# A transformer block with expert routing on one core: pool waits tile by tile, a rearranged start of the gate loop, and a third buffer for stored gates

## The chip, the cores and the metric

The kernel runs on one core of a Trainium2 chip. The metric is the device time of one execution in microseconds (us); lower is better. The engines are TensorE (PE, with its weight loads shown as PEld), VectorE (DVE), ScalarE (ACT), GpSimd (POOL) and SyncE (SP, which only issues transfers). SP, ACT and POOL each issue transfers from their own queue.

## The reference

`x` is 512 tokens of 1024 values. A first half mixes tokens, a second sends each token to experts:

```python
xn = rms_norm(x, ln_mix_g); proj = xn @ w_in
a_out = gmlp_spatial_gating(...)          # 8 groups, blocks of 128 tokens
b_out = banded_chunk_attention(...)       # 8 heads, relative bias
x = x + concat([a_out, b_out]) @ w_out
# PEER, per token, 8 heads: two 128-wide score rows, top 16 of each, best 16 of the sums
s_top, i_top = top_k(sc, 16); best, pos = top_k(pairwise sums, 16)
g = softmax(best); eidx = i0 * 128 + i1   # 16 of 16384 experts for each head
h = gelu(einsum(expert_u[eidx], xb))
out = x + einsum(g * h, expert_v[eidx])
```

## The kernel before

All arithmetic is float32; a product of float32 matrices is made as three fp32r products of a high and a low part (`mm3`, L190). The high part comes from an ACT copy (L154), the low part from a subtraction on DVE or POOL (L155), both in `load_split` (L146). It has three raw, five high and five low buffers.

The four token tiles of 128 are not treated alike. Tile 0 fetches its experts' rows by index ("gathers", L1105 to L1120). The other three tiles multiply with **all** 16384 experts: 128 blocks of 128 experts, two blocks to a chunk, 64 chunks. Of these three tiles, the last 64 tokens get their `expert_u` products by gathers too ("early" gathers, L649 to L669, 64 of them with the row product at L662), so the dense product over `expert_u` has only 320 columns (`multiply_some`, L690; one block is 24 matmuls). Its results wait in `act` tiles, 23 chunks ahead (`AHEAD`).

The order of the work is:

1. Mixing (to about 240 us), in pools `prea`, `preb`, `prec`, opened one after the other in the same memory.
2. Routing (240 to 427 us, loop at L882): for each head the query product, the score product, top 16, candidate sums, choice. Beside it the early gathers and some dense blocks run. `indices_early(h)` (L665) writes eight columns of one index tile `eui`, by a POOL transfer (L668) and a POOL cast (L669); six gathers follow each head's. At the end stand softmax (L796), `indices_of` (L862), two held splits, the last `indices_early`, and `dots_early(0)`, which orders all remaining row products.
3. The gate loop (L1017, 48 steps and 2 of lead, each for 8 tokens), in an order written out by hand for PE, DVE, ACT and POOL. A step makes a one-hot product `bm` on POOL (L963), a one-hot `am` on DVE (L971), 8 matmuls of `bm` and `am` (L979), two ACT copies into `gst` (L982), and after every two steps a 1 MB store to DRAM from the ACT queue (L986). `gst` has two buffers. Dense blocks, one early gather in two of three steps, and the row products stand between. A gate group is read back by `load_gates` (L991). The first two loads of it are POOL transfers.
4. The output (from about 592 us, L1182): for each chunk 36 matmuls of 512 columns into six PSUM banks (`second_product`, L1137), the dense blocks of the chunk 23 further on, and between them tile 0's routing (`route_gathered`, L1087, at every third chunk, eight times; its scores come by a transfer into `sc0`, one buffer) and tile 0's 256 gathers. DVE and ACT instructions are ordered by a planner with priorities, PE by hand.

Memory that a closed pool leaves is given to later pools. As written, the first use of it waits for the whole earlier pool's work. DMA issues of POOL use a descriptor scratch of 16 KB in each partition.

Of the kernel before, what the change touches and what calls it, by code (L numbers as in the profile page):

```python
# [80 lines left out]
GB = 8  # L81
TC = 8
# [10 lines left out]
def hybrid_block(tc, x, ln1, w_in, gng, wsT, bsb, qkg, bias, w_out, ln2, wq, skT, uT, ud, vd, out):  # L93
    nc = tc.nc
    ctx = ExitStack()
    with ctx:
# [26 lines left out]
        roots, behind_scale, behind_norm = [], [], []  # L123
# [22 lines left out]
        def load_split(src, eng=nc.vector, **dims):  # L146
# [125 lines left out]
        with tc.tile_pool(name="prea", bufs=1) as prea:  # L272
# [144 lines left out]
        with tc.tile_pool(name="preb", bufs=1) as preb:  # L417
# [163 lines left out]
        xbp = ctx.enter_context(tc.tile_pool(name="xbp", bufs=1, side="right"))  # L581
# [8 lines left out]
        with tc.tile_pool(name="prec", bufs=1) as preb:  # L590
# [27 lines left out]
        ps_x = ctx.enter_context(tc.tile_pool(name="ps_x", bufs=1, space=PSUM))  # L618
        ps_a = ctx.enter_context(tc.tile_pool(name="ps_b", bufs=4, space=PSUM))
# [5 lines left out]
        rt = ctx.enter_context(tc.tile_pool(name="rt", bufs=1, side="right"))  # L625
# [4 lines left out]
        actp = ctx.enter_context(tc.tile_pool(name="actp", bufs=1, side="right"))  # L630
# [4 lines left out]
        gat = gat_ctx.enter_context(tc.tile_pool(name="gat", bufs=1, side="right"))  # L635
        xbu = px()
        routing = ExitStack()
        rq = routing.enter_context(tc.tile_pool(name="rq", bufs=1))
# [5 lines left out]
        eui = gat.tile([P, HS], I32, name="eui")  # L644
# [4 lines left out]
        def gather_early(n, rows_of, n_rows):  # L649

            for j in early[:n]:
                row = rows_of.tile([P, D], F32, name="rowe", tag="rowe", bufs=n_rows)
                nc.gpsimd.indirect_dma_start(out=row, out_offset=None, in_=ud,  # L653
                                             in_offset=bass.IndirectOffsetOnAxis(ap=eui[:, j:j + 1], axis=0))
# [10 lines left out]
        def indices_early(h):  # L665

            js = slice(h * HK, (h + 1) * HK)
            nc.gpsimd.dma_start(eui[0:P - UX, js], eidx[P - UX:P, TT - 1, h * TOPK + HK:(h + 1) * TOPK])  # L668
            nc.gpsimd.tensor_copy(eui[P - UX:P, js], eidx[P - UX:P, TT - 1, h * TOPK:h * TOPK + HK])  # L669
# [212 lines left out]
        for h in range(NH + 1):  # L882
# [7 lines left out]
            if h > 1:  # L890
# [34 lines left out]
        indices_early(NH - 1)  # L925
        ready_early(NH - 1)
        dots_early(0)
# [5 lines left out]
        more.append(ctx.enter_context(tc.tile_pool(name="more", bufs=1)))  # L933
        gp_ctx = ExitStack()
        gp = gp_ctx.enter_context(tc.tile_pool(name="gp", bufs=1))
# [74 lines left out]
        with tc.manual_schedule(engines=engines):  # L1010
            gather_early(1, gat, ROWA)
# [5 lines left out]
            for n in range(steps + LEAD):  # L1017
# [31 lines left out]
                if n == own - 1:  # L1049
# [3 lines left out]
                    gcp = [ctx.enter_context(tc.tile_pool(name="gcp", bufs=1, side="right"))]  # L1053
# [24 lines left out]
        ep = ctx.enter_context(tc.tile_pool(name="ep", bufs=1))  # L1078
# [58 lines left out]
        def second_product(c):  # L1137
# [5 lines left out]
            for b in range(BC):  # L1143
                bb = (c * BC + b) % GB
                av = act[:, b, :].rearrange("p (n t) -> p n t", t=TG)
                nc.vector.tensor_tensor(av, av, gc[:, 0:NDU // TG, bb, :], op=ALU.mult)
            nc.scalar.activation(wh[:, :, 0:NDU], act, AF.Copy)
            mark = nc.vector.tensor_tensor(wl[:, :, 0:NDU], act, wh[:, :, 0:NDU].bitcast(F32), op=ALU.subtract)
            if c == 1:
# [98 lines left out]
```

## Time and profile before

| | |
|---|---|
| three runs | 1442.33 us median (1438.95 to 1442.57) |
| the profiled execution | 1436.48 us, of which the span from the first to the last instruction is 1434.4 us |
| granted TensorE clock over the span | 0.993 |
| busy share of the span | PE 97%, PEld 86%, DVE 80%, POOL 49%, ACT 43% |

All rows further down are of this one profiled execution. "Idle before" is time in which the engine did nothing ahead of an instruction, with what ended it; a wait is given as total, times, longest.

### The profile page before, as it was taken

To read this page: it belongs to the slowest core of one execution; us is meant where nothing else is said; L and a number is where in the kernel's file an instruction comes from. 1 tells how busy PE (TensorE), PEld (TensorE's weight loads), DVE (VectorE), ACT (ScalarE), POOL (GpSimd) and SP (SyncE) were. 2 spreads that over 40 slices of the span, in tenths; PEclk is the share of its full clock that TensorE was granted. 3 is DMA by queue.
4 is the path that set the end of the run, shared out by engine and by line. 5 is a ranking of instruction groups with operands and counts; after the bars stand their busy time and mean duration, and the time that the engine had idled before them with its cause. 6 is when DMAs were issued, how large, how long until landed. Compare 5 with 4: busy or idle time off the path is not lost.

```text
span 1434.4 us, 21711 instructions
## 1 busy us (share of the span) xinstructions
PE 1391.9 (97%) x7838; PEld 1229.5 (86%) x7838; DVE 1150.5 (80%) x2502; ACT 611.4 (43%) x957; POOL 700.6 (49%) x487
## 2 busy tenths in 40 slices
PE   9999999999987978999999999999999999999998
PEld 7887788898986978898988898998998998888887
DVE  5537755998996888599999999889879888688883
ACT  5447635434442434554543444343333333333331
POOL 0002104678769988424554646545546455254520
PEclk9999999999998999999999999999999999999999
DMA  4352225667667998988998999999999989689981
GB/s 168 126 191 74 89 104 191 206 229 276 216 225 248 300 313 251 294 296 310 332 351 312 339 349 368 347 389 356 376 339 359 361 326 378 243 326 353 340 332 70
DMA packets 164330, 396.24 MB, mean 276 GB/s; under 512 B 12880, under 2 KB 75232, under 8 KB 162176
## 3 DMA queue, kind: packets, MB, share of 16 engines
q1 hardware_dynamic: 64640, 194.14, 37.6%
q0 software_dynamic: 48176, 173.46, 32.9%
q10 hardware_dynamic: 51408, 27.27, 6.6%
q8 instruction: 61, 1.00, 0.3%
q14 instruction: 45, 0.37, 0.1%
HBM read 363.34 MB, written 31.46 MB: 275 GB/s over the span
## 4 chain that ended last, share of the span: by engine, by line
PE 76%; DVE 9%; POOL 5%; DMA 4%; issue 3%; ACT 2%; another core or an unknown queue 0%; ACTq 0%; POOLq 0%; DVEq 0%; SPq 0%
PE pa L1168 22%; PE px L1168 11%; PE pu L194 9%; PE pu L192 9%; PE pu L193 9%; PE pa L192 4%; PE pa L979 3%; PE pa L193 3%; PE pa L194 3%; POOL bm L963 2%; POOL rowe L653 1%; DMA gd<-gst 1%; DVE lo L155 1%; POOL lo L155 1%; DVE row L1109 1%
## 5 line engine op out<-in xcount | busy, mean ns | idle before, releaser
L154 ACT ACTIVATE hi<-raw 128x1024 fp32r<-128x1024 f32 x296 | 312.8, 1058 | 468.5 <-DMA raw<-in_vd 124.0
L155 DVE TENSOR_TENSOR lo<-raw,hi 128x1024 fp32r<-128x1024 f32 x241 | 295.8, 1229 | 78.3 <-ACT hi L154 76.0
L1107 POOL DMA_INDIRECT row<-in_ud,eint x128 | 199.0, 1555 | 193.6 <-DVE acc L1120 129.8
L1118 POOL DMA_INDIRECT row<-in_vd,eint x128 | 180.6, 1411 | 165.3 <-DVE row L1109 110.9
L194 PE MATMUL pu<-xch,lo 128*128 128x320 f32 x784 | 244.7, 312 | 8.1 <-POOL lo L155 4.9
L192 PE MATMUL pu<-xch,hi 128*128 128x320 f32 x784 | 248.9, 317 | 2.0 <-ACT act L716 2.0
L193 PE MATMUL pu<-xcl,hi 128*128 128x320 f32 x784 | 244.2, 311 | 0.0
L1168 PE MATMUL pa<-lo,wh 128*128 128x512 f32 x512 | 199.7, 390 | 0.0
L1168 PE MATMUL pa<-hi,wh 128*128 128x512 f32 x512 | 199.3, 389 | 0.0
L155 POOL TENSOR_TENSOR lo<-raw,hi 128x1024 fp32r<-128x1024 f32 x55 | 131.4, 2403 | 98.3 <-ACT hi L154 95.7
L1120 DVE SCALAR_TENSOR_TENSOR acc<-row,hw,acc 128x1024 f32<-128x1024 f32 x128 | 164.9, 1288 | 2.0 <-DMA row<-in_vd,eint 1.9
L1109 DVE SCALAR_TENSOR_TENSOR row<-row,xb 128x1024 f32<-128x1024 f32 x128 | 157.8, 1235 | 1.7 <-DMA row<-in_ud,eint 1.7
L1168 PE MATMUL pa<-hi,wl 128*128 128x512 f32 x512 | 158.4, 389 | 0.0
L194 PEld LDWEIGHTS pu<-xch,lo 128*128 128x128 f32 x784 | 149.2, 190 | 8.9 <-POOL lo L155 5.4
L192 PEld LDWEIGHTS pu<-xch,hi 128*128 128x128 f32 x784 | 149.5, 191 | 4.1 <-ACT act L716 2.5
L193 PEld LDWEIGHTS pu<-xcl,hi 128*128 128x128 f32 x784 | 149.5, 191 | 1.7
L979 PE MATMUL pa<-bm,am 128*128 128x128 f32 x768 | 97.3, 280 | 19.0 <-POOL bm L963 12.9
L1168 PEld LDWEIGHTS pa<-hi,wh 128*128 128x128 f32 x512 | 96.1, 188 | 20.6
L1168 PEld LDWEIGHTS pa<-lo,wh 128*128 128x128 f32 x512 | 96.1, 188 | 20.3
L1168 PEld LDWEIGHTS pa<-hi,wl 128*128 128x128 f32 x512 | 96.1, 188 | 20.2
L979 PEld LDWEIGHTS pa<-bm,am 128*128 128x128 f32 x768 | 92.2, 194 | 23.7 <-POOL bm L963 17.2
L1168 PE MATMUL px<-hi,wh 128*128 128x512 f32 x256 | 100.5, 393 | 3.3 <-ACT hi L154 3.3
(236 smaller groups left out, 2629.4 us busy)
## 6 DMA issues: line engine op xcount, KB each, us to landing
raw<-in_uT SPq DMA_DIRECT2D x128, 512.0 KB
raw<-in_vd SPq DMA_DIRECT2D x128, 512.0 KB
gd<-gst ACTq DMA_DIRECT2D x24, 1024.0 KB
gc<-gd SPq DMA_DIRECT2D x15, 1280.0 KB
raw<-in_w_in SPq DMA_DIRECT2D x19, 512.0 KB
raw<-in_wq SPq DMA_DIRECT2D x16, 512.0 KB
raw<-in_w_out SPq DMA_DIRECT2D x8, 512.0 KB
gc<-gd SPq DMA_DIRECT2D x15, 256.0 KB
```

Source lines behind the costliest of these rows:

```text
L154: nc.scalar.activation(hi, raw, AF.Copy)
L155: ins = eng.tensor_tensor(lo, raw, hi.bitcast(F32), op=ALU.subtract)
L192: nc.tensor.matmul(ps, lh[0], rh[0], start=first, stop=False)
L193: nc.tensor.matmul(ps, lh[0], rh[1], start=False, stop=False)
L194: nc.tensor.matmul(ps, lh[1], rh[0], start=False, stop=last)
L963: nc.gpsimd.tensor_tensor(bm.rearrange("p t (h l) -> p t h l", l=BL), d[0][:, ts_, :, None].to_broadcast(full), d[1][:, ts_, None, :].to_b ...
L979: nc.tensor.matmul(ps[:, i * P:(i + 1) * P], am[:, 4 * q + i, :], bm[:, 4 * q + i, :], start=True, stop=True)
L1107: nc.gpsimd.indirect_dma_start(out=row, out_offset=None, in_=ud, in_offset=bass.IndirectOffsetOnAxis(ap=eint[:, j:j + 1], axis=0))
L1109: nc.vector.scalar_tensor_tensor(row, row, 1.0, xb0, op0=ALU.mult, op1=ALU.mult, accum_out=hw[:, j:j + 1])
L1118: nc.gpsimd.indirect_dma_start(out=row, out_offset=None, in_=vd, in_offset=bass.IndirectOffsetOnAxis(ap=eint[:, j:j + 1], axis=0))
L1120: nc.vector.scalar_tensor_tensor(acc0, row, hw[:, j:j + 1], acc0, op0=ALU.mult, op1=ALU.add)
L1168: nc.tensor.matmul(accs[t][half], (wh, wh, wl)[k][:, b, tok], w[b][k % 2][:, ds_], start=first and k == 0, stop=last and k == 2)
```

## The change

Fourteen pools get `reuse_waits="tile"`: a tile in memory that an earlier pool left waits for the tiles whose bytes it takes, and no longer for the whole pool. `eui` becomes eight tiles, one for each head. The last pass of the routing loop no longer makes head 6's indices and issues no gathers, and behind it neither head 7's indices nor the remaining row products stand: the indices of both heads are made in steps 1 and 2 of the gate loop, six gathers are issued behind the last held split, the loop's gathers start at step 2 in three of four steps, and a step does at most one row product, from step 1 on. `gst` gets a third buffer, `sc0` a second, and the descriptor scratch shrinks to 4 KB. In chunk 0 of the output the products go by token tile, the dense blocks of chunk 23 are put ahead of the last token tile's, and the gates of the last tokens are split only there; the scaling products of chunks 1 to 3 are queued behind the chunk before.

```diff
+SCRATCH = 4096
@@ load_split
-            nc.scalar.activation(hi, raw, AF.Copy)
+            top = nc.scalar.activation(hi, raw, AF.Copy)
             ins = eng.tensor_tensor(lo, raw, hi.bitcast(F32), op=ALU.subtract)
+            halved[:] = [getattr(i, "ins", i) for i in (top, ins)]
@@ prea, preb, xbp, prec, ps_x, ps_b, rt, actp, gat, rq, more, gp, gcp, ep alike
-        with tc.tile_pool(name="prea", bufs=1) as prea:
+        with tc.tile_pool(name="prea", bufs=1, reuse_waits="tile") as prea:
@@ early gathers
-        eui = gat.tile([P, HS], I32, name="eui")
+        eui = [gat.tile([P, HK], I32, name=f"eui{h}") for h in range(NH)]
-        def dots_early(lag):
-            while len(issued) > lag:
+        def dots_early(lag, most=NH * HK):
+            while len(issued) > lag and most > 0:
+                most -= 1
@@ routing loop and its end
-            if h > 1:
+            if 1 < h < NH:
                 with tc.issue_after(splits[0]):
                     indices_early(h - 2)
                     ready_early(h - 2)
                     gather_early(EARLY, gat, ROWA)
@@
         for _ in range(HELD):
             split_next()
-        indices_early(NH - 1)
-        ready_early(NH - 1)
-        dots_early(0)
+        with tc.issue_after(splits[0]):
+            gather_early(EARLY, gat, ROWA)
@@ gate loop
-            gather_early(1, gat, ROWA)
             multiply_tile()
@@
-                        st = gp.tile([P, NB, TG], F32, name="gst", tag="gst", bufs=2)
+                        st = gp.tile([P, NB, TG], F32, name="gst", tag="gst", bufs=3)
@@
-                if n < own - 7 and n % 3 < 2:
+                if n in (1, 2):
+                    indices_early(NH - 3 + n)
+                    ready_early(NH - 3 + n)
+                if n:
+                    dots_early(LAGE, 1)
+                if 1 < n < own - 7 and n % 4 != 1:
                     gather_early(1, gat, ROWA)
-                dots_early(LAGE)
@@ route_gathered
-            sc = ep.tile([P, n, 2, NK], F32, name="sc0", tag="sc0", bufs=1)
+            sc = ep.tile([P, n, 2, NK], F32, name="sc0", tag="sc0", bufs=2)
@@ second_product(c, between)
+            with queued_behind(marked if c < GB // BC else []):
+                for b in range(BC):
+                    ...
+                    nc.vector.tensor_tensor(av, av, gc[:, 0:NDU // TG, bb, :], op=ALU.mult)
+            if c:
+                with queued_behind(own_last if c < GB // BC else []):
+                    last_tokens()
-            if c == NCHK - 1:
+            if c in (0, NCHK - 1):
                 order.sort(key=lambda bt: bt[1])
-            for b, t in order:
+            for i, (b, t) in enumerate(order):
+                if c == 0 and i == BC * (ND - 1):
+                    between()
+                    with queued_behind(halved):
+                        last_tokens()
@@ kernel
-    nc = bacc.Bacc("TRN2", target_bir_lowering=False, num_devices=1)
+    nc = bacc.Bacc("TRN2", target_bir_lowering=False, num_devices=1, dynamic_dma_scratch_size=SCRATCH)
```

`last_tokens()` holds the two instructions that split the gates of the last 64 tokens (L1157, L1158 before), and `between()` the dense blocks of the chunk 23 further on; for the other chunks both stand where they stood.

## Rows read from the trace of the kernel before

**Rows 1.** The head of the page: busy time and share of the span; and PE in 40 equal slices of 35.9 us, in tenths.

```profile
PE 1391.9 (97%) x7838; PEld 1229.5 (86%) x7838; DVE 1150.5 (80%) x2502; ACT 611.4 (43%) x957; POOL 700.6 (49%) x487
PE   9999999999987978999999999999999999999998
```

**Rows 2.** All waits of PE over the span that are 2.5 us or more in total: engine, tile and line, what it waited for, total us, times, longest.

```profile
PE pa L979 <- POOL bm L963: 12.9, 13, 2.9
PE pa L979 <- ACT gst L982: 5.9, 2, 3.0
PE pu L194 <- POOL lo L155: 4.9, 1, 4.9
PE px L1168 <- ACT hi L154: 3.3, 1, 3.3
PE pu L194 <- DVE lo L155: 3.3, 1, 3.3
PE pu L192 <- ACT act L716: 2.5, 2, 2.0
```

**Rows 3.** Stretches of the span: length, then busy us (and instructions) of PE, PEld, DVE, ACT, POOL, the granted clock, the DMA share and GB/s.

```profile
426.30:445.10 18.80, 11.85 (x68) 11.10 (x67) 16.24 (x33) 3.45 (x6) 14.65 (x12) 0.82 0.59 196
442.30:553.60 111.30, 93.69 (x723) 89.12 (x722) 87.73 (x144) 47.09 (x81) 100.68 (x60) 0.98 0.91 285
553.60:591.80 38.20, 36.83 (x311) 36.39 (x311) 24.48 (x34) 20.92 (x38) 31.21 (x17) 1.00 0.89 256
591.80:606.20 14.40, 11.12 (x62) 10.50 (x61) 8.95 (x16) 6.55 (x11) 2.20 (x4) 0.88 0.96 310
606.00:760.00 154.00, 150.75 (x830) 135.94 (x828) 144.11 (x418) 73.89 (x112) 65.50 (x47) 1.00 0.84 311
760.00:780.00 20.00, 20.00 (x99) 18.55 (x100) 19.05 (x30) 6.12 (x11) 12.94 (x9) 0.86 0.93 349
```

**Rows 4.** In order of time at the end of routing: PE (the first two rows are 24 matmuls apart), ACT, POOL. Start us, duration us, engine, line, operation; in brackets the idle time before and its releaser.

```profile
422.78 0.31 PE L194 MATMUL pu<-xbh,lo 128*128 128x320 f32 x1
426.30 0.31 PE L194 MATMUL pu<-xbh,lo 128*128 128x320 f32 x1
434.06 0.64 PE L194 MATMUL pu<-xch,lo 128*128 128x320 f32 x1 [4.88 <-POOL lo L155]
...
420.88 1.06 ACT L154 ACTIVATE hi<-raw 128x1024 fp32r<-128x1024 f32 x1 [2.11 <-DMA raw<-in_uT]
...
427.18 0.19 POOL L669 CAST eui<-eidx 64x8 int32<-64x8 f32 x1 [5.69 <-DMA rowe<-in_ud,eui]
431.42 4.91 POOL L155 TENSOR_TENSOR lo<-raw,hi 128x1024 fp32r<-128x1024 f32 x2
442.33 1.94 POOL L963 TENSOR_TENSOR bm<-hb,lb 128x1024 f32<-128x1024 f32 x1
```

**Rows 5.** DVE in order of time over the same stretch: the first and the last of six row products, the last copy of the choice, and the last of the digits that `bm` reads; then DVE's waits for such rows from 395 to 620 us.

```profile
422.95 1.22 DVE L662 SCALAR_TENSOR_TENSOR rowe<-rowe,px 128x1024 f32<-128x1024 f32 x1
...
435.88 1.27 DVE L662 SCALAR_TENSOR_TENSOR rowe<-rowe,px 128x1024 f32<-128x1024 f32 x1
437.08 0.24 DVE L792 COPY eidx<-tree 128x48 f32<-128x48 f32 x1
440.59 0.41 DVE L952 TENSOR_TENSOR lb<-iota_k,pa 128x256 f32<-128x256 f32 x1
...
DVE rowe L662 <- DMA rowe<-in_ud,eui: 1.5, 2, 1.1
```

**Rows 6.** Waits in the gate loop, 442 to 554 us.

```profile
ACT gst L982 <- DMA gd<-gst: 27.2, 9, 6.1
POOL dots L680 <- DVE dots L679: 3.6, 1, 3.6
POOL lo L155 <- ACT hi L154: 3.2, 1, 3.2
```

**Rows 7.** The early gathers on POOL: two that follow one another, the view of line L653 from 440 to 600 us (shortest, median, longest in ns), and of all index transfers.

```profile
401.12 0.94 POOL L653 DMA_INDIRECT rowe<-in_ud,eui  x1 [0.30 <-issue]
402.37 0.94 POOL L653 DMA_INDIRECT rowe<-in_ud,eui  x1 [0.30 <-issue]
L653 POOL DMA_INDIRECT rowe<-in_ud,eui x21: 978/982/1790, 444.4 to 543.3; - x21
L668 POOL DMA_DIRECT2D eui<-eidx x8: 545/570/586, 257.8 to 439.8; - x8
```

**Rows 8.** The passage from the loop to the output, in order of time: ACT (the first split of the output), POOL, PE and DVE.

```profile
599.20 1.36 ACT L1147 ACTIVATE wh<-act 128x640 fp32r<-128x640 f32 x2 [3.76 <-DMA gd<-gst]
599.66 0.59 POOL L996 DMA_DIRECT2D gc<-gd  x1 [13.00 <-DMA gd<-gst]
601.89 0.79 PE L1168 MATMUL px<-hi,wh 128*128 128x512 f32 x1 [3.28 <-ACT hi L154]
607.92 1.20 DVE L155 TENSOR_TENSOR lo<-raw,hi 128x1024 fp32r<-128x1024 f32 x1
```

**Rows 9.** The stall in the output at 756 us: SP's transfer of tile 0's scores, DVE, PE.

```profile
748.94 0.33 SPq L1091 DMA_DIRECT2D sc<-s0d  x1
755.40 0.49 DVE L732 MAX8 top<-sc 128x8 f32<-128x128 f32 x2 [4.29 <-DMA sc<-s0d]
759.98 0.63 PE L194 MATMUL pu<-xch,lo 128*128 128x320 f32 x1 [3.25 <-DVE lo L155]
```

More of the change, by code (lines that the diff above doesn't have):

```diff
@@ L414, in hybrid_block @@
                                          scale=qkgt[:, half:half + 1])
-        with tc.tile_pool(name="preb", bufs=1) as preb:
+        with tc.tile_pool(name="preb", bufs=1, reuse_waits="tile") as preb:
             wst_t = preb.tile([P, 8, P], F32, name="wst_t")
@@ L578, in hybrid_block @@
         pre_ctx.close()
-        xbp = ctx.enter_context(tc.tile_pool(name="xbp", bufs=1, side="right"))
+        xbp = ctx.enter_context(tc.tile_pool(name="xbp", bufs=1, side="right", reuse_waits="tile"))
         xch = xbp.tile([P, KT, NDU], F32R, name="xch")
@@ L587, in hybrid_block @@
         xbd = dram.tile([2, P, D], F32, name="xbd")
-        with tc.tile_pool(name="prec", bufs=1) as preb:
+        with tc.tile_pool(name="prec", bufs=1, reuse_waits="tile") as preb:
             g2row = preb.tile([P, D], F32, name="g2row")
@@ L629, in hybrid_block @@
         hw = rt.tile([P, NH * TOPK], F32, name="hw")
-        actp = ctx.enter_context(tc.tile_pool(name="actp", bufs=1, side="right"))
+        actp = ctx.enter_context(tc.tile_pool(name="actp", bufs=1, side="right", reuse_waits="tile"))
         acts = {}
         gat_ctx = ExitStack()
-        gat = gat_ctx.enter_context(tc.tile_pool(name="gat", bufs=1, side="right"))
+        gat = gat_ctx.enter_context(tc.tile_pool(name="gat", bufs=1, side="right", reuse_waits="tile"))
         xbu = px()
         routing = ExitStack()
-        rq = routing.enter_context(tc.tile_pool(name="rq", bufs=1))
+        rq = routing.enter_context(tc.tile_pool(name="rq", bufs=1, reuse_waits="tile"))
         row = gat.tile([P, D], F32, name="rowe", tag="rowe", bufs=ROWA)
@@ L932, in hybrid_block @@
         gds = [dram.tile([NB // GB, P, n1 - n0, GB * TG], F32, name=f"gd{n0}") for n0, n1 in GROUPS]
[L933 removed]
+        more.append(ctx.enter_context(tc.tile_pool(name="more", bufs=1, reuse_waits="tile")))
         gp_ctx = ExitStack()
[L935 removed]
+        gp = gp_ctx.enter_context(tc.tile_pool(name="gp", bufs=1, reuse_waits="tile"))
         def gates_of(t, ff):
@@ L1052, in hybrid_block @@
                     gat_ctx.close()
-                    gcp = [ctx.enter_context(tc.tile_pool(name="gcp", bufs=1, side="right"))]
+                    gcp = [ctx.enter_context(tc.tile_pool(name="gcp", bufs=1, side="right", reuse_waits="tile"))]
                 if n == steps - 2:
@@ L1075, in hybrid_block @@
         gp_ctx.close()
-        ep = ctx.enter_context(tc.tile_pool(name="ep", bufs=1))
+        ep = ctx.enter_context(tc.tile_pool(name="ep", bufs=1, reuse_waits="tile"))
         gcp.append(ep)
@@ L1182, in hybrid_block, with ahead @@
             for c in range(NCHK):
-                with tc.high_priority(offset=PRIO):
-                    mark = second_product(c)
+                def ahead():
                     if c + AHEAD < NCHK:
@@ L1187, in hybrid_block @@
                             pass
+                with tc.high_priority(offset=PRIO):
+                    mark = second_product(c, ahead)
+                    if c:
+                        ahead()
                 if c % ROUTE == 0 and c < PARTS * ROUTE:
```

35 lines of the change are left out of this document (18 added, 17 removed).

## The prediction

> **What bounds the kernel now.** I read the head of the page first, then PE's waits, then the stretches in which PE isn't full. PE is busy 1391.9 of 1434.4 us, so 42.5 us are idle, and the slices show where: the passage from routing to the gate loop, the loop, and its end; the output is full but for one slice [rows 1]. The list of PE's waits says the same: 12.9 us for POOL's one-hot products, 5.9 for ACT's copies of gates, and four smaller entries of 2.5 to 4.9 us [rows 2]. Summed over the stretches PE idles 7.0 us at the end of routing (426.3 to 445.1), 17.6 in the gather half of the loop (442.3 to 553.6, overlapping the first by 2.8), 1.4 in its second half, 3.3 behind it and 3.3 around 757 [rows 3]. A PE that has waited comes back at a lower clock: granted 0.82 in the first of these, 0.88 behind the loop, 0.86 from 760 to 780, where the engine is full. At the lower of two levels (half speed) 0.86 over 20 us is 5.6 us at half speed, 2.8 us of lost work; so a wait of 3.3 us costs about 6. Everything else is PE at its own pace, so only these places can give time, at most the 42.5 us and what the clock held back behind them.
>
> **Reference for the sum.** The profiled execution took 1436.48 us (span 1434.4). The three runs' median is 1442.33, 5.85 above it. I take the gains from the profile and subtract them from the median.
>
> **A, the end of routing.** PE's last routing block starts at 426.30; then it waits 2.0 us for ACT and 4.88 for POOL's subtraction [rows 2, 4]. POOL was late because its cast of the indices waited 5.69 us for a gather still reading the one index tile, with three more gathers behind it ahead of the subtraction. ACT's last high part for it was done at 421.9 [rows 4]; with eight tiles and no index work here, the last subtraction (4.91 us for two, so 2.5) can end by 425, and this wait goes. What is late next is DVE: `bm` number 0 starts at 442.33, after the digits (end 441.0), after `eidx` (437.08). Six row products stand in that chain: 1.22 us each less the overlap with the next, 1.15, so 6.9, and 1.5 us of waiting for their rows, 8.4 together [rows 5]. Moved behind the loop's start they leave `eidx` at 428.7 and the digits at 432.6. The second index pair goes from ahead of `bm` on POOL too. POOL itself: subtractions done at 425, then six gathers at 1.25 us from start to start [rows 7], 7.5 us, so 432.5: just free. So `bm` 0 could start 9.7 us earlier. PE needs three blocks and four transposes before the first gate product, 9.1 us at full clock (a block's 24 matmuls take 3.52 us [rows 4], 0.147 each), so it would be there at 436 instead of 445. Above: 9.7. Below: 4.9, the one POOL wait, if ACT's softmax and the raw loads hold the rest. I take 8, nearer the chain that I can follow instruction by instruction.
>
> **B, the loop.** To 553.6 it runs at POOL's pace: POOL is busy 100.68 of 111.30 us, and each gather has a gap of issue beside that. Its true stalls are 3.2 us for ACT (which stood behind a copy waiting for a store) and 3.6 for a DVE copy, 6.8 together [rows 3, 6]. ACT's 27.2 us of waits for stores come from two `gst` buffers, and the third takes them away. New on POOL's path are one gather more after `bm` 0 (22 for 21, 1.25 us) and two index pairs (0.57 for the transfer and 0.19 for the cast, 1.5 both [rows 4, 7]). So 111.3 becomes 107.2 at best: +4. Below: 0, if the stores' transfers are the limit and not the buffer. I take 3. The six row products that A frees land on DVE here: 7 us against 23.6 us of DVE idleness in the stretch [rows 3], covered; without that cover they would cost their 7 us. The second half runs at PE's pace and gives nothing.
>
> [...] The row: DMA's share is 0.91 over the stretch and 0.89 after it [rows 3], so transfers are nearly full while 24 stores, 22 gathers and the block loads share them. [...] My own bound from rows: 0.59 of 18.8 us plus 0.91 of 111.3 us is 112.4 us of transfers for the 127.3 us from 426.3 to 553.6, so A and B together can't pass 14.9; 11 fits, but leaves little.
>
> **C, loop to output.** PE stops at 598.6 and begins the output at 601.89; ACT's first `wh` stood 3.76 us for the last stores, which it does not read: the pool wait. With waits tile by tile it can go at 595.4, where ACT fell idle. The gates of the last 64 tokens really need the last store (POOL's load waited 13 us for it) [rows 8]; that is now needed only for the third token tile, after 24 matmuls of 512 columns (0.147 x 512 / 320 = 0.235 us each, 5.6) and two dense blocks. What is late next: these blocks are pulled ahead of 12 products, and the second one's low part ended at 609.1 [rows 8]. PE would want it at 598.6 + 5.6 + 3.5 = 607.7, so 1.4 us can come back as a new wait. Above: 3.3 + 1.7 us of slow clock (0.88 of 14.4) = 5. Below: 0, if `wh` lies in bytes of `gst`. I take 3.
>
> **D, the second score buffer.** At 751 DVE stood 4.29 us for scores whose transfer SP could issue only at 748.94, when the one buffer was free; the dense block's low part came late, PE waited 3.25 us and lost 2.8 to the clock [rows 3, 9]. With two buffers the load is free to go a route earlier, three chunks before its use. Gain 6; above 6.1, below 0, if DVE, busy 144 of 154 us in this stretch, is late anyway.
>
> **Nothing for** the waits of the pools before 400 us: PE's slices are full there [rows 1], so earlier transfers are hidden behind PE's own queue; of the 42.5 us the five sums leave 10 for all other places, the start and the tail among them, and that bounds it. The scratch costs nothing that I can see in rows, with its bound under the rivals. [...]
>
> Sum: 8 + 3 + 3 + 6 = 20. Against the profile 1416.5, against the median 1422.
>
> **Rivals.**
> (1) The transfers rule the loop: the time won at its start returns as ACT's waits for stores, because 0.91 is already the limit. For it: the share, and 27.2 us of store waits with two buffers. Against: the output from 606 on moves 311 GB/s at a share of 0.84, the loop 285 at 0.91, so a share near 1 is no fixed rate [rows 3, 6]. A and B give nothing, C and D stay: 1442 - 9 = 1433. [...]
> (2) DVE rules the output. For it: 144 of 154 us. Against: PE had no wait there but one [rows 2]. Then C and D fall to nothing, and 1442 - 11 = 1431.
> (3) The other side: the quarter-size scratch makes POOL's indirect transfers wait for room. Place: POOL's path in the gate loop. The shortest gather issue there is 978 ns, the longest 1790 [rows 7]; if all 28 took the longest, 28 x 0.81 = 22.7 us stand on the path that sets the loop: 1442 - 20 + 23 = 1445. It decides from 0.71 us for each gather (20 / 28). The output's 256 gathers have slack on POOL (half idle). Against: at most six gathers are ever in flight, by the row buffers.
> (4) The change doesn't do what it says: the planner orders DVE and SP in the output anew, and another queue's head waits where `sc` did, and the loop's ends shift alike. A gives 5, lost again in the new order: no change, 1440.
>
> **How the numbers follow.** Forecast 0.62, (1) 0.12, (2) 0.08, (3) 0.10, (4) 0.08. A difference of 0.3%, 4.3 us, is about what a measurement of this kernel can tell. Faster holds the forecast, (1) and (2): 0.82; same 0.08; slower 0.10. The forecast's own range: the upper bounds sum to 9.7 + 4 + 5 + 6.1 = 24.8, and 5 more for the pools' earlier starts and the spread of runs: 1412; the lower ones to 4.9: 1437. For 8 in 10 I set 1410 to 1438, which takes in (1) and (2) and leaves out (3), (4) and a little below.
>
> **What would show it.** A: no POOL wait at the index cast, `bm` 0 near 433, PE's wait for POOL's subtraction gone. B: ACT's waits for stores under 8 us in the loop, and the time from the first `bm` to the last gather 107 us, with `bm` the releaser still. C: `wh` before 597. D: no DVE wait over 1 us for `sc`, and PE full from 606 on. Wrong would make it: gathers over 1.2 us in the loop, a DMA share of 1.0 with store waits unchanged, or new waits of PE in the output.

## The result, and the profile after

The changed kernel takes 1430.1 us (median of 7 runs, 1424.71 to 1436.54) against 1440.08 (7 runs, 1436.6 to 1442.57) of the kernel before on the same chip: a ratio of 0.9931, 95% interval 0.9912 to 0.995. It was faster, as forecast, and inside the range, but by 10 us where the sum said 20. The profiled execution took 1427.15 us (span 1425.1), 9.3 less than before.

The head of the page and PE's slices: the 12th (end of routing) is full now, of the loop's and its end's the 13th, 15th and 16th are not [rows 1].

```profile
PE 1390.5 (98%) x7838; PEld 1229.4 (86%) x7838; DVE 1152.2 (81%) x2502; ACT 614.3 (43%) x957; POOL 705.3 (49%) x487
PE   9999999999998988999999999999999999999998
```

PE's waits over the span. POOL's one-hot products lead more than before, ACT's copies of gates and POOL's last subtraction have gone, and a wait for ACT's `act` of up to 3.4 us and one for DVE's `gate` are new [rows 2].

```profile
PE pa L980 <- POOL bm L964: 16.2, 11, 2.5
PE pu L194 <- ACT act L718: 4.4, 2, 3.4
PE px L1187 <- ACT hi L155: 1.6, 1, 1.6
PE pa L196 <- POOL lo L156: 1.5, 1, 1.5
PE pa L943 <- DVE gate L685: 1.5, 1, 1.5
```

The stretches, columns as in [rows 3]: routing's last 18.7 us, the gather half of the loop, its second half, the passage to the output, the output to 760 us, and the 20 us behind; last, the passage of the kernel before over the same length.

```profile
418.10:436.80 18.70, 17.86 (x124) 17.63 (x123) 17.36 (x56) 7.08 (x11) 15.86 (x12) 1.00 0.78 277
432.80:543.00 110.20, 98.04 (x766) 95.26 (x765) 94.97 (x157) 51.17 (x87) 103.10 (x66) 0.97 0.95 304
543.00:584.20 41.20, 35.02 (x276) 33.86 (x275) 29.72 (x34) 18.50 (x33) 31.19 (x17) 0.96 0.77 220
584.20:622.00 37.80, 31.81 (x176) 29.58 (x175) 28.94 (x113) 17.31 (x28) 6.49 (x8) 0.91 0.76 261
622.00:760.00 138.00, 138.00 (x760) 124.73 (x760) 133.99 (x342) 66.68 (x100) 74.74 (x48) 1.00 0.90 333
760.00:780.00 20.00, 20.00 (x107) 17.70 (x106) 18.27 (x30) 8.24 (x13) 6.97 (x6) 1.00 0.99 381
...
591.80:629.60 37.80, 34.52 (x195) 31.88 (x194) 31.26 (x105) 19.62 (x31) 3.54 (x7) 0.95 0.82 279
```

PE idles 0.8 us at the end of routing (7.0 before) and 12.2 in the loop's gather half (17.6 before), but 6.2 in its second half (1.4 before) and 6.0 in the passage (3.3 before). The end of routing in order of time, POOL and DVE, answers to [rows 4, 5]:

```profile
432.83 3.83 POOL L964 TENSOR_TENSOR bm<-hb,lb 128x1024 f32<-128x1024 f32 x2 [1.15 <-DVE lb L953]
437.24 0.19 POOL L671 CAST eui<-eidx 64x8 int32<-64x8 f32 x1
...
428.70 0.25 DVE L794 COPY eidx<-tree 128x48 f32<-128x48 f32 x1
432.28 0.41 DVE L953 TENSOR_TENSOR lb<-iota_k,pa 128x256 f32<-128x256 f32 x1
```

To place the gain I cut each profiled execution at events all kernels share: the last copy into `eidx`, the first `bm`, the issue of the last store of gates, the span's end. "Loop" is from first `bm` to last store, "rest" from there to the end. Kernels with the same instructions in the same order reach `eidx` up to 4.2 us apart (428.70 and 432.94, the changed kernel and `e1_gst2`), so stretches from an event on say more here than spans. "Held" is what VectorE's weight splits in the loop (over 1.2 us each) and its one product of gates and dots (over 0.29) took above their undisturbed times, an excess under 0.4 us left out; it is the subject of half the experiments.

| kernel | eidx | first bm | last store | span | loop | rest | held |
|---|---|---|---|---|---|---|---|
| before | 437.08 | 442.33 | 591.78 | 1434.4 | 149.5 | 842.6 | 3.4 |
| changed | 428.70 | 432.83 | 584.22 | 1425.1 | 151.4 | 840.9 | 9.2 |
| changed, again (e12) | 430.42 | 434.55 | 585.00 | 1424.1 | 150.5 | 839.1 | 9.4 |
| e1_gst2 | 432.94 | 437.08 | 588.40 | 1428.3 | 151.3 | 839.9 | 4.6 |
| e2_chunk0 | 430.33 | 434.46 | 585.79 | 1426.0 | 151.3 | 840.2 | 8.9 |
| e3_sc1 | 429.49 | 433.62 | 585.21 | 1423.1 | 151.6 | 837.9 | 8.1 |
| e4_gate_psum | 429.45 | 433.57 | 585.80 | 1426.7 | 152.2 | 840.9 | 4.6 |
| e5_routing_alone | 429.96 | 434.12 | 589.85 | 1435.0 | 155.7 | 845.2 | 9.4 |
| e6_poolwaits | 428.65 | 432.81 | 582.55 | 1424.3 | 149.7 | 841.8 | 7.8 |
| e7_scores_first | 429.66 | 433.79 | 583.65 | 1422.9 | 149.9 | 839.3 | 8.3 |
| e8_split_dve | 429.43 | 433.57 | 584.23 | 1423.2 | 150.7 | 839.0 | 12.3 |
| e9_no_lock | 430.38 | 434.51 | 579.98 | 1420.0 | 145.5 | 840.0 | 0 |
| e10_no_lock_gst2 | 428.44 | 432.57 | 590.00 | 1428.9 | 157.4 | 838.9 | 0 |
| e11_both | 427.87 | 432.00 | 579.74 | 1418.3 | 147.7 | 838.6 | 1.3 |

The changed kernel's 9.3 us are 9.5 at the first `bm`, 1.9 lost in the loop, 1.7 won in the rest. The forecast had 8, 3 and 9.

Where the loop loses: one operation of DVE, a product of 64 partitions by 128, and what POOL ran beside it; then the same two of the kernel before.

```profile
546.49 7.32 DVE L685 TENSOR_TENSOR gate<-gate,dots 64x128 f32<-64x128 f32 x1 [0.37 <-ACT dots L684]
553.84 1.22 DVE L972 TENSOR_TENSOR am<-iota_k,pa 128x1024 f32<-128x1024 f32 x1
545.63 2.39 POOL L156 TENSOR_TENSOR lo<-raw,hi 128x1024 fp32r<-128x1024 f32 x1
547.94 5.71 POOL L964 TENSOR_TENSOR bm<-hb,lb 128x1024 f32<-128x1024 f32 x3
```
```profile
559.76 2.00 DVE L683 TENSOR_TENSOR gate<-gate,dots 64x128 f32<-64x128 f32 x1 [2.98 <-ACT dots L682]
559.68 3.87 POOL L963 TENSOR_TENSOR bm<-hb,lb 128x1024 f32<-128x1024 f32 x2
```

A product of an eighth of `am`'s row length takes six times `am`'s time, and ends 0.2 us behind the end of POOL's run of four operations (553.65); before, it ended about where the first of POOL's `bm` did. Everything on DVE behind it, `am` for PE first, is 7 us late.

### The profile page after: what moved, and what is told of

Same layout as the page of the kernel before. It is cut to its first block, busy times and chain, and to the rows that moved or that the text cites. A ratio compares the mean times of both kernels' runs of the same rounds, so it can differ in the third digit from the quotient of the medians.

```text
span 1425.1 us, 21665 instructions
## 1 busy us (share of the span) xinstructions
PE 1390.5 (98%) x7838; PEld 1229.4 (86%) x7838; DVE 1152.2 (81%) x2502; ACT 614.3 (43%) x957; POOL 705.3 (49%) x487
## 4 chain that ended last, share of the span: by engine, by line
PE 56%; DVE 0%; issue 0%
PE pa L1187 24%; PE px L1187 12%; PE pu L194 7%; PE pu L195 7%; PE pu L196 7%; DVE res L1225 0%
## 5 line engine op out<-in xcount | busy, mean ns | idle before, releaser
L1122 POOL DMA_INDIRECT row<-in_vd,eint x128 | 184.2, 1439 | 173.1 <-DVE row L1113 118.8
L1113 DVE SCALAR_TENSOR_TENSOR row<-row,xb 128x1024 f32<-128x1024 f32 x128 | 157.2, 1231 | 0.1
L1187 PE MATMUL px<-hi,wh 128*128 128x512 f32 x256 | 100.2, 391 | 1.6 <-ACT hi L155 1.6
```

The costliest lines, as they stand in the source:

```text
L1113: nc.vector.scalar_tensor_tensor(row, row, 1.0, xb0, op0=ALU.mult, op1=ALU.mult, accum_out=hw[:, j:j + 1])
L1122: nc.gpsimd.indirect_dma_start(out=row, out_offset=None, in_=vd, in_offset=bass.IndirectOffsetOnAxis(ap=eint[:, j:j + 1], axis=0))
L1187: nc.tensor.matmul(accs[t][half], (wh, wh, wl)[k][:, b, tok], w[b][k % 2][:, ds_], start=first and k == 0, stop=last and k == 2)
```

## The experiments

### Each edit undone

**`e1_gst2`**: two buffers of stored gates.

```diff
-st = gp.tile([P, NB, TG], F32, name="gst", tag="gst", bufs=3)
+st = gp.tile([P, NB, TG], F32, name="gst", tag="gst", bufs=2)
```

> The changed kernel with two buffers for stored gates instead of three; everything else as changed. By the prediction's sum (part B) the third buffer gives the loop 3 us, so this kernel is 3 us slower than the changed one: about 0.995 of the kernel before, and ACT's copies into the stored gates wait again for stores (27.2 us in six waits before). By the reading of the changed kernel's trace (GpSimd works 19.1 to 19.3 of each 20 us from 440 to 540 us, so it and not the store buffers sets the loop's step) the buffer gives at most 1 us: 0.993 to 0.994, dots' transfer on GpSimd within 1 us of 542.96 and the last stored gate within 1.5 us of 584.22, with or without waits on ACT.

Measured: 1431.85 us (12 runs), 0.9938 [0.9916, 0.9961]. The instructions of every engine stand in the changed kernel's order. ACT's waits for stores are back, 31.9 us in 11 (27.2 before, in nine [rows 6] and not in six), PE waits 3.4 us for ACT's copies; yet the loop is 151.3 us, the changed kernel's 151.4. The two differ inside it: up to POOL's transfer of dots the loop takes 112.6 us here and 110.1 there, behind it 38.7 and 41.3, and DVE's product of gates and dots took 0.68 us here and 7.32 there. So the third buffer gave 2.5 us up to that transfer, near the 3 of the sum, and they were lost again behind it. In time the kernel is 4 to 6 us above `e2`, `e3` and `e4`, which have three buffers and ran on the same chip (1425.55 to 1427.69), and 2 to 6 above the changed kernel's two medians, which are of other chips.

**`e2_chunk0`**: the output's first chunk as before.

```diff
-if c in (0, NCHK - 1):
+if c == NCHK - 1:
     order.sort(key=lambda bt: bt[1])
...
-if c == 0 and i == BC * (ND - 1):
-    between()
-    with queued_behind(halved):
-        last_tokens()
```

> The changed kernel with the output's first chunk as it was before: its products go b by b, the last tokens' gates are split ahead of them, and the dense products of chunk AHEAD follow the whole chunk; no ordering between its vector operations. By the prediction's sum (part C) the rearranged chunk gives 3 us, so this kernel is 3 us slower than the changed one: 0.995 of the kernel before, with PE waiting about 3 us for the last tokens' split near 593 to 595 us. By the reading of the changed kernel's trace the rearranged chunk costs 3 to 5 us (PE stands 3.4 us for ScalarE's act at 603 to 607 us, 1.0 us at 616 us, and its clock is granted 0.83 from 600 to 620 us), so this kernel is 2 to 5 us faster than the changed one: 0.990 to 0.992, and PE is full from about 600 us on.

Measured: 1427.69 us (6 runs), 0.9919 [0.9891, 0.9947]: neither 3 us slower nor clearly faster. In its 37.8 us from the last store on PE idles 6.3 us, in the changed kernel 6.0, before 3.3. The order of the chunk decides what PE waits for, not how long. With the old one:

```profile
595.43 0.50 PE L1181 MATMUL px<-lo,wh 128*128 128x512 f32 x1 [1.41 <-DVE lo L156]
599.31 0.50 PE L1181 MATMUL pa<-hi,wh 128*128 128x512 f32 x1 [1.08 <-ACT wh L1167]
615.01 0.63 PE L194 MATMUL pu<-xch,hi 128*128 128x320 f32 x1 [3.28 <-ACT act L718]
```

**`e3_sc1`**: one buffer for the routing's scores.

```diff
-sc = ep.tile([P, n, 2, NK], F32, name="sc0", tag="sc0", bufs=2)
+sc = ep.tile([P, n, 2, NK], F32, name="sc0", tag="sc0", bufs=1)
```

> The changed kernel with one buffer for the stored scores of the routing (sc0) instead of two. By the prediction's sum (part D) the second buffer gives 6 us: this kernel is 6 us slower than the changed one, 0.997 of the kernel before, with DVE waiting some 4 us for the transfer of the scores near 750 us, PE standing some 3 us after it, and the granted clock near 0.86 in the 20 us that follow. If the stall were gone by the earlier end of the loop alone, it would be as fast as the changed kernel, 0.993.

Measured: 1425.55 us (6 runs), 0.9899 [0.9875, 0.9923], no slower than the changed kernel, and PE is full from 620 to 1400 us. The stall of [rows 9] does not come back, though the load is as late as before: SP issues the last scores 157.5 us after the last store of gates (157.2 before). What moved is DVE's order: its first operation on them comes at 755.38 without a wait, 170.2 us after the store, where before it stood ready at 159.3 (755.40 less 4.29). With two buffers (changed kernel) DVE turns to them at 730.43, 146.2 us after the store, and SP had issued them at 694.99. So the buffer does what was forecast, and an order that asks later does as well without it. SP and DVE in this run:

```profile
742.66 0.33 SPq L1095 DMA_DIRECT2D sc<-s0d  x1
...
755.38 0.29 DVE L734 MAX8 top<-sc 128x8 f32<-128x128 f32 x1
```

**`e5_routing_alone`** (edit: of the diff, only routing's end, the index tiles by head and the loop's begin; the rest as in the kernel before).

> The kernel before with the edits of routing's end and of the loop's beginning alone (row products out of routing's last step, index tiles by head, gathers issued ahead of the loop, the last two heads' indices inside it); pool-wide waits, a 16 KB scratch, two buffers of stored gates, one of sc0, the output's first chunk as before. By the prediction's sum this part (A) is worth 8 us and the rest 12: 1432 of 1440 us, 0.994, some 5 us slower than the changed kernel as measured. By the reading of the traces so far (from the last copy into eidx to the span's end: 997.3 us before, 996.4 changed) A is all that the change gives: 0.993, as fast as the changed kernel within 2 us, with the first one-hot products of GpSimd near 433 us and with DVE's wait for the scores near 740 us back if the tile by tile waits had removed it, gone if the scores' earlier issue had.

Measured: 1434.08 us (12 runs), 0.9959 [0.9936, 0.9982], some 6 us won of the 8 forecast for A, and 4 and 8 us behind the changed kernel's two medians (1430.1 and 1426.24), which are of other chips. The first `bm` is at 434.12, so the edit does at routing's end what it did in the changed kernel; its loop is 6.2 us longer than before's, with three operations of DVE held (2.5, 2.5 and 4.4 us) and 31.5 us of store waits. The stall for the scores is there (DVE 3.5 us), with one buffer as in `e3` but before's order of DVE.

**`e6_poolwaits`** (edit: `reuse_waits="tile"` taken out of every pool).

> The changed kernel with pool-wide waits in all pools; every other edit stays (4 KB scratch, three buffers, two of sc0, rearranged chunk). By the prediction the tile by tile waits give nothing by themselves: 0.993, and no wait of over 2 us more than in the changed kernel. If they carry the changed kernel's shorter routing's end or its output, this is 3 to 9 us slower: 0.995 to 0.999.

Measured: 1428.34 us (7 runs), 0.9921 [0.9889, 0.9953]: no slower than the changed kernel. ACT's first `wh` waits 3.7 us for the stores again, as in [rows 8], and PE idles 7.6 us in the passage instead of 6.0; the loop is as quick. The tile by tile waits gave an earlier start of the output and nothing that could be seen in the time.

### The held operation

**`e4_gate_psum`**: one operand of DVE's product in PSUM.

```diff
-nc.scalar.activation(dots[own], dots[own], AF.Gelu_apprx_tanh)
-nc.vector.tensor_tensor(gate[own, TT - 1, :], gate[own, TT - 1, :], dots[own]..., op=ALU.mult)
+hot = pa()[own, 0:NH * TOPK]
+nc.scalar.activation(hot, dots[own]..., AF.Gelu_apprx_tanh)
+nc.vector.tensor_tensor(gate[own, TT - 1, :], gate[own, TT - 1, :], hot, op=ALU.mult)
```

> The changed kernel with GELU of the early dots written into a PSUM tile, so that VectorE's product of gates and dots (64 partitions x 128) reads one operand from PSUM and not both from SBUF. Theory 1: a VectorE operation that reads two SBUF operands does not get on while GpSimd runs one of its own (in the changed kernel it took 7.32 us and ended 0.2 us behind GpSimd's three one-hot products; before it took 2.00 us and ended with GpSimd's operation too): then it takes under 0.5 us here, the one-hot after it starts near 547 us instead of 553.84, and the kernel gains 2 to 4 us, 0.990 to 0.992 of the kernel before. Theory 2: it is long for another reason (it waits for something that the records do not show): it stays over 5 us and the time stays 0.993.

Measured: 1426.64 us (6 runs), 0.9902 [0.9877, 0.9928]. The product takes 0.29 us: theory 1. The gain in the loop did not come, for another operation of the same kind was caught, a weight split that reads `raw` and `hi` in SBUF (1.22 us undisturbed):

```profile
529.54 4.58 DVE L156 TENSOR_TENSOR lo<-raw,hi 128x1024 fp32r<-128x1024 f32 x1
529.23 3.81 POOL L964 TENSOR_TENSOR bm<-hb,lb 128x1024 f32<-128x1024 f32 x2
533.19 1.79 POOL L655 DMA_INDIRECT rowe<-in_ud,eui  x1 [0.16 <-issue]
```

It began 0.3 us behind POOL's pair of `bm`, ended at 534.12, 1.1 us behind their end, and the gather next to it took 1.79 instead of 0.98. In the changed kernel the same split began 0.7 us ahead of POOL's `bm`, and took 1.22:

```profile
528.38 1.22 DVE L156 TENSOR_TENSOR lo<-raw,hi 128x1024 fp32r<-128x1024 f32 x1
529.10 2.29 POOL L964 TENSOR_TENSOR bm<-hb,lb 128x1024 f32<-128x1024 f32 x1
```

**`e8_split_dve`**: two splits from POOL to DVE.

```diff
-split_next(nc.vector if split % 3 and n > 5 else nc.gpsimd)
+split_next(nc.vector if split % 3 else nc.gpsimd)
```

> The changed kernel with two weight splits at the loop's beginning (2.38 us each on GpSimd) given to VectorE (1.22 us each where nothing holds them). Theory 1, GpSimd sets the loop's step: it has 4.8 us less to do, dots' transfer comes 3 to 5 us earlier after the first one-hot product (110.1 us in the changed kernel), and the time goes down as much: 0.990 to 0.991. Theory 2, two-operand operations of VectorE in SBUF are held up by GpSimd's: VectorE's two splits take 2.4 to 5 us each instead of 1.22, GpSimd's operations or gathers next to them grow, and the gain is under 2 us: 0.992 to 0.994.

Measured: 1425.05 us (6 runs), 0.9897 [0.9862, 0.9932]. POOL has 4.8 us less to split, and the transfer of dots comes 110.3 us after the first `bm`, as with the changed kernel's 110.1, for POOL idles 10.9 us on the way and not 7.1: theory 2 for the loop. Of the two moved splits one took 2.96 us and one 1.40; three operations were held 12.3 us in all (1.8, 3.4, 7.2). The time by itself lies nearer theory 1, and its interval reaches into both.

**`e9_no_lock`**: `e4`'s edit, and no DVE operation of the loop with two tensors in SBUF.

```diff
+other = plain[0] if plain and eng is nc.vector else hi.bitcast(F32)
-ins = eng.tensor_tensor(lo, raw, hi.bitcast(F32), op=ALU.subtract)
+ins = eng.tensor_tensor(lo, raw, other, op=ALU.subtract)
```

> The changed kernel with GELU of the early dots in a PSUM tile, and with the weight splits that VectorE makes inside the loop subtracting a PSUM tile (xbu) in place of the rounded half in SBUF: the splits' low halves are then not those of the reference, the work is as long. So no operation of VectorE in the loop reads two tensors from SBUF. Theory 1, the changed loop gives its gain back in such operations (9.2 us above their undisturbed times in the changed kernel, 3.4 us before): none of them is over 1.4 us here, and the stretch from the first one-hot product of GpSimd to the last store, 151.4 us in the changed kernel, goes to 142 to 146 us; the kernel to 0.986 to 0.989. Theory 2, GpSimd's own work (some 135 us in that stretch) sets it and hides these delays: it stays within 2 us of 151.4.

Measured: 1422.25 us (6 runs), 0.9873 [0.9849, 0.9898]; the loop 145.5 us, inside theory 1's range and 5.9 us below the changed kernel's. In the loop `plain` holds `xbu`, a tile in PSUM, so DVE's splits subtract that, and their low parts are not those of the reference. The splits also no longer wait for ACT's `hi`, which in the changed kernel is 0.6 us ahead of the transfer of dots and 2.2 behind it; `e11` keeps the latter wait and takes the same time behind the dots (38.3 us, here 38.4). DVE's splits and POOL's gathers in the loop, shortest, median and longest in ns; then the gathers of the changed kernel:

```profile
L158 DVE TENSOR_TENSOR lo<-raw,px x5: 1212/1212/1216, 480.0 to 563.3; 128x1024 fp32r<-128x1024 f32 x5
L657 POOL DMA_INDIRECT rowe<-in_ud,eui x23: 947/983/1021, 430.0 to 532.2; - x23
```
```profile
L655 POOL DMA_INDIRECT rowe<-in_ud,eui x22: 979/986/1907, 440.5 to 533.4; - x22
```

**`e10_no_lock_gst2`** (edit: `e9` with two buffers of stored gates).

> The kernel of the run above with two buffers of stored gates in place of three: the third buffer's worth where nothing holds VectorE up. By the prediction's part B the same stretch is some 3 us longer than above. If the loop's step is set elsewhere (GpSimd), it is within 1 us of the one above.

Measured: 1429.24 us (6 runs), 0.9916 [0.989, 0.9942], 7 us above `e9`, and the loop 157.4 us, 11.9 longer; its rest is shorter. Where nothing holds DVE up, the third buffer is worth the most; PE stands for ACT's copies, which stand for stores. The first row is ACT's, the second PE's, both from 430 to 592 us:

```profile
ACT gst L985 <- DMA gd<-gst: 35.1, 10, 7.7
PE pa L982 <- ACT gst L985: 8.9, 3, 4.5
```

That it is longer than `e1`'s loop (151.3), where DVE was held 4.6 us, is one execution each, and left open.

### The passage, and a quicker version

**`e7_scores_first`**: in the changed kernel the passage reads, ACT, POOL, DVE and PE in turn:

```profile
602.79 0.22 ACT L760 ACTIVATE top<-pos 128x16 f32<-128x16 uint32 x1 [6.38 <-DVE pos L738]
606.60 0.41 ACT L718 ACTIVATE act<-pu 128x320 f32<-128x320 f32 x1
592.34 0.58 POOL L997 DMA_DIRECT2D gc<-gd  x1 [13.27 <-DMA gd<-gst]
593.98 0.55 POOL L1095 DMA_DIRECT2D sc<-s0d  x1
600.78 0.49 DVE L734 MAX8 top<-sc 128x8 f32<-128x128 f32 x2 [3.10 <-DMA sc<-s0d]
607.07 0.64 PE L194 MATMUL pu<-xch,hi 128*128 128x320 f32 x1 [3.38 <-ACT act L718]
```

```diff
-load_gates(0, nc.gpsimd, range(1, len(GROUPS)))
...
+early_sc = {0: scores(0, nc.gpsimd)}
 xb0 = ep.tile([P, D], F32, name="xb0")
 nc.gpsimd.dma_start(xb0, xbd[0])
 acc0 = ep.tile([P, D], F32, name="acc0")
 nc.gpsimd.dma_start(acc0, x2d[0])
+load_gates(0, nc.gpsimd, range(1, len(GROUPS)))
```

> The changed kernel with three transfers on GpSimd's queue (the scores of the first route, xb, acc) issued ahead of the second load of gates, which stands 13.27 us for the last stores; nothing else moves. Theory: the stall at 601 to 607 us (TensorE for ScalarE's act, which stands behind ScalarE's top, which waits 6.38 us for VectorE's pos, which waits 3.10 us for the scores that were issued at 593.98 us behind the gates) comes from this order: then the scores land before 592 us, ScalarE's wait for pos goes below 1 us, TensorE is busy 18 or more of 20 us from 600 to 620 us at a clock of 0.9 or more, and the kernel gains 3 to 6 us: 0.989 to 0.991 of the kernel before. Rival: TensorE has next to wait for the last tokens' gates, which come no earlier: then the gain is under 1 us, 0.993.

Measured: 1427.56 us (6 runs), 0.9909 [0.9874, 0.9945], not told from the changed kernel. ACT's wait for `pos` goes from 6.38 to 3.19 us and PE's wait at 607 us is gone, but PE now waits 2.0 us for `act` at 589 us and 1.9 for `hi` at 597 (1.6 in the changed kernel); it idles 5.0 us in the 37.8 behind the last store, against 6.0 and 5.4 in the changed kernel's two executions. The queue's order was a cause of that one stall; most of the passage's loss is elsewhere.

**`e11_both`** (edits: `e4` and `e7` together) and **`e12_changed_again`** (no edit), on one chip:

> A version meant to be quicker than both: the changed kernel with GELU of the early dots in PSUM and with the first route's scores, xb and acc issued ahead of the second load of gates; it computes all that the reference asks. By the two runs that made one of these edits each (from the last copy into eidx to the span's end 996.4 us in the changed kernel; 997.2 with the first edit, 993.2 with the second), 2 to 4 us faster than the changed kernel: 0.988 to 0.991 of the kernel before.

> The changed kernel once more, on the chip of the three above, so that they can be set beside it: 0.991 to 0.995 of the kernel before.

Measured: `e11_both` 1421.35 us (5 runs, 1420.35 to 1424.7), 0.9871 [0.9847, 0.9895]; the changed kernel 1426.24 (6 runs, 1425.37 to 1431.53), 0.9908 [0.9885, 0.9932]. The runs of the two don't overlap: 5 us won. By the table 2.7 of the spans' 5.8 us are in the loop (held 1.3 instead of 9.4), 2.5 fall ahead of `eidx`, where the two do the same and which counts for nothing, and 0.5 in the rest.

## Why the prediction was right, and the gain half of what it said

**The bound.** Right: only the places with idle PE moved, and the first 400 us gave nothing (the last copy into `eidx` but one starts at 418.11, before at 418.52).

**A, 8 us: right.** Each step came at the named time: `eidx` at 428.70 (428.7 forecast), `lb` ended at 432.69 (432.6), `bm` at 432.83 (433), no wait at the cast, PE's wait for POOL's subtraction gone. That the times agree to a tenth is luck, for executions differ by up to 4 us here; the gain is not. From the last copy into `eidx` but one to the first `bm` it is 23.8 us before and 14.7 or 14.8 in all thirteen executions with this edit, and to PE's first gate product 26.6 and 18.6 or 18.7: 9.1 us for POOL and 7.9 for PE. (The 9.1 us put down for PE's "three blocks" are 60 matmuls, two and a half blocks, and four transposes.)

**B, 3 us: the buffer's worth near it, two other steps wrong, -1.9 in all.** ACT's waits for stores in the gather half are none (27.2 before [rows 6]), and `bm` stayed the releaser. Divided at POOL's transfer of dots, the loop reads so, in us ("product" is DVE's of gates and dots):

| kernel | to the dots | of it POOL busy | POOL idle | behind the dots | product |
|---|---|---|---|---|---|
| before | 111.3 | 100.7 | 10.6 | 38.2 | 2.00 |
| changed | 110.1 | 103.1 | 7.1 | 41.3 | 7.32 |
| changed, again (e12) | 110.1 | 103.1 | 7.0 | 40.4 | 7.19 |
| e1_gst2 | 112.6 | 103.0 | 9.6 | 38.7 | 0.68 |
| e4_gate_psum | 113.9 | 103.0 | 10.9 | 38.3 | 0.29 |
| e7_scores_first | 109.5 | 102.5 | 7.0 | 40.3 | 7.36 |
| e9_no_lock | 107.1 | 100.2 | 7.0 | 38.4 | 0.29 |
| e10_no_lock_gst2 | 116.1 | 100.3 | 15.8 | 41.4 | 0.29 |
| e11_both | 109.4 | 102.4 | 7.0 | 38.3 | 0.29 |

*Up to the dots* the sum said 107.2, and 110.1 was measured. The step that failed: the sum took away two stalls of POOL, 3.2 us for ACT and 3.6 for DVE's copy of dots. The first has gone. The second stands, with 2.8 us, because the copy still comes behind DVE's last row products; 107.2 and 2.8 are 110.0. POOL starts 0.07 us behind the copy's end, as before (553.54 and 553.61); the view names a matmul that ended about then. (The sign's "107 us" was put down to the last gather; the sum's 111.3 and 107.2 run to the transfer of dots.)

```profile
541.44 1.22 DVE L665 SCALAR_TENSOR_TENSOR rowe<-rowe,px 128x1024 f32<-128x1024 f32 x1
542.70 0.19 DVE L681 COPY dots<-du 64x64 f32<-64x64 f32 x1
542.96 0.78 POOL L682 DMA_DIRECT2D dots<-du  x1 [2.82 <-PE pa L980]
```

That `e9` has 107.1 is chance: it keeps this stall (2.7 us) and lacks something that the sum had left in its base, POOL's own operations that take longer beside a split of VectorE. These cost POOL 3.0 us before and 2.9 in the changed kernel (three gathers of 1.8 to 1.9 us for 0.98, one `bm` of 2.29 for 1.94), 2.2 in `e7` and `e11`, 0 in `e9`, and where POOL idles 7.0 or 7.1 us they are nearly all that parts the kernels. Where one split alone was held 3.4 us (`e4`, `e8`), POOL idles 3.8 us more. The third buffer by itself, from `e1` to the changed kernel, is worth 2.5 us here, all of it idle time of POOL.

*Behind the dots* the sum said nothing, and 3.1 us were lost. The step that failed: I took durations of DVE in the loop as fixed and asked only whether DVE had idle time (the six row products were "covered"). Where the product took at most 2.00 us this stretch is 38.2 to 38.7 (before, `e1`, `e4`, `e9`, `e11`), where it took 4.67 or more 40.3 to 41.3 (the changed kernel twice, `e2`, `e3`, `e5` to `e8`). `e10` alone does not fit: 41.4 with 0.29, and stores waited for.

The prices were there to be seen in the page of before: one `gate` of 2.00 us, and [rows 7]'s longest gather of 1790 ns. I read that number as the scratch's worst price (rival 3); `e9` shows what it is, for without two-operand operations no gather of the loop is above 1021 ns. The sum in the column "held" of the first table does not order the loops: with three buffers and 4.6 to 12.3 us held they take 149.7 to 152.2. Which operation was caught was settled by tenths of a us between two engines (a split 0.3 us behind POOL's `bm` took 4.58 us in `e4`, one 0.7 us ahead 1.22 in the changed kernel). That the cost of a held operation depends on who waits behind it is my reading; no run takes the two apart.

The least that I allowed for this term was 0, if the stores' transfers and not the buffer were the limit. The runs don't bear that out: the buffer is worth 2.5 us up to the dots from `e1` to the changed kernel and 9.0 from `e10` to `e9` (11.9 of loop, 7 us of time). The share is 0.95 at 304 GB/s with three buffers against 0.91 at 285 before [rows 3], so 0.91 was not the limit.

**C, 3 us: wrong, -4.3, and some -2.5 in the second execution.** `wh` went at 587.99 (before 597, as forecast), 3.8 us after the last store instead of 7.4. But PE idles 6.0 us in the passage (3.3 before) at a clock of 0.91 (0.95 before over as long a stretch); in `e12` it idles 5.4 at 0.95. I allowed 1.4 us for the pulled dense blocks, waiting for their low part; they wait for their PSUM's `act`, 3.4 and 1.0 us, which stands on ACT behind the first route's `top`, which waits for the scores, which POOL issues behind the load that waits for the last store. I named that 13 us wait and did not ask what else was queued behind it. `e2` and `e7` show that neither this order nor the chunk's is the whole: PE idles 5 to 6 us with either. What sets the passage beyond that stays open; `e5`, with the old passage, and `e3`, with the new one, both idle 4.0.

**D, 6 us: right in the changed kernel, but not for the buffer alone.** The stall at 756 us is gone with its clock (1.00 from 760 to 780, 0.86 before; there the trace grants 0.50 in each us from 759 to 765 and 1.00 from 766 on, and a matmul of 320 columns takes 0.63 us and then 0.31), so PE's 3.3 us of idle and the 2.8 of clock are won, and the scores are loaded a route ahead, as the step said. `e3` shows that the second buffer isn't the only way to it: there the planner put DVE's first operation on the scores 11 us later, and nothing was lost. Which of the other edits made the planner do so (`e5`, with none of them, kept the stall) wasn't tried. The sign "no DVE wait over 1 us for `sc`" did not hold to the letter: waits of 3.1 us at 600.8, in the passage, and of 1.1 at 666.4 stand.

**Rivals.** (1) fell: store waits went and the share rose to 0.95. (2) fell: DVE is 133.99 of 138 us busy and PE full. (3) fell by its own test: the median gather is 986 ns (982 before), and the long ones have another cause, for `e9`, with the same scratch, has none above 1021. (4) fell as a forecast of no change; that DVE's order in the output can move with edits made elsewhere, `e3` showed. Two of the signs named for being wrong came nevertheless: gathers over 1.2 us in the loop (1.79, 1.79 and 1.91), which were there before and are not the scratch's, and new waits of PE in the output (3.4 and 1.0 us), which are C's.

**The sum.** 9.5 - 1.9 - 4.3 + 6 = 9.3, D put in at its forecast and C being the rest's 1.7 less D. Two of the four terms, B and C, came out below the least that was allowed for them, 0; the total stayed in the range because A and D came whole. The four terms were added as if independent. That B's and C's gains were lost because A had brought the engines closer together is not shown; that `e5`, with A alone, has a loop 6.2 us longer than before fits it.

## What to carry to other kernels

Before pricing work as covered on an engine, look through its shortest-to-longest durations: an operation whose longest is far above its median may be waiting for something that no semaphore shows (here a gather's 1790 ns against 982). And before a stall is taken out of a sum, look at what the stalled operation needs: only what the change makes earlier goes. Where VectorE works beside a GpSimd as full as this one (busy 103.1 of 110.2 us), try one operand in PSUM for its elementwise operations: here a product went from 7.32 to 0.29 us (`e4`), and with the splits' operand as well the loop from 151.4 to 145.5 (`e9`). For a queue that stands at a transfer for data still being stored, list what is behind it, and put what doesn't depend on that data ahead (here that removed one stall, and no time that could be told).

## What the runs showed of the hardware

In this loop VectorE's operations on two SBUF tensors were long where they began while a `bm` or a split of GpSimd had 0.5 us or more still to run: 7.32 us against 0.29 (`e4`, one operand in PSUM) for the product, 4.58 (`e4`) against 1.22 for a split. In the kernel before and in the changed one five splits began 0.6 to 1.5 us behind the begin of such a `bm`; they took 1.58 to 2.47 us, and each ended 1.09 us behind that `bm`. A gather did not do this: the changed kernel's split at 528.38 began 0.3 us behind one of 0.99 us and took 1.22. Operations of the same loop with one operand in PSUM were never long: the changed kernel's 48 `am` take 1206 to 1222 ns, its 28 row products 1207 to 1215.

The order of the two engines went with it: 0.7 us ahead of GpSimd's `bm` a split took 1.22 us, 0.3 us behind it 4.58. And the operation did not get in between GpSimd's instructions: the product ended behind four in a row (546.49 to 553.81, GpSimd until 553.65), and it was as long in `e3`, `e12`, `e7` and `e8` (7.16, 7.19, 7.36 and 7.46 us).

GpSimd's operations were longer too, where VectorE came first: in the kernel before and in the changed one each of the loop's five gathers over 1.1 us (1.79 to 1.91, with a median of 0.98 and 0.99) overlaps a split of VectorE, even where the split took its 1.22 us, and each of the five `bm` over 2 us (2.29 to 2.92, 1.93 to 1.94 in the median) begins beside a split that is running. In `e9`, where no split of VectorE in the loop has two SBUF tensors, the longest gather takes 1.02 us, and the `bm` at 563.61, beside a split that began at 563.3, 1.93; the changed kernel's at 570.08, beside one that began at 569.77, took 2.71. The changed kernel's longest gather:

```profile
478.27 1.22 DVE L156 TENSOR_TENSOR lo<-raw,hi 128x1024 fp32r<-128x1024 f32 x1
478.44 1.91 POOL L655 DMA_INDIRECT rowe<-in_ud,eui  x1 [0.16 <-DVE lb L953]
```
